# A sparse-attention kernel whose index scores take their second matmul on half of the array's rows, two heads at a time

## The chip, the core and the metric

The kernel runs on one core of a Trainium2 chip. TensorE (PE in the profile) multiplies matrices on an array of 128 rows and 128 columns: a weight load (PEld) brings one operand into the array, a matmul streams the other through it and writes to PSUM, which has 8 banks here of 128 x 512 float32. VectorE (DVE), ScalarE (ACT) and GpSimd (POOL) work on elements; SyncE (SP) and other engines issue DMAs. The metric is the device time of one execution in microseconds (us); smaller is better. The kernel before takes 1685.8 us (median of 3 runs, 1685.49 to 1687.46).

## The reference

One layer on 512 frames with 2048 channels: a norm, one wide projection, a sparse-attention mixer, a retention mixer, gates, output projections and a final norm. The change touches the part that scores keys for the sparse attention. Each query has 16 index heads of 64 numbers, all heads share one key of 64 numbers per frame, and the 128 best keys of each query are kept:

```python
score = jnp.einsum('bqhd,bsd->bqsh', qi_c, ki)
index = jnp.einsum('bqsh,bqh->bqs', jax.nn.relu(score), w_c).astype(jnp.float32)
admissible = jnp.arange(L) < limit
index = jnp.where(admissible[None, None, :], index, -jnp.inf)
_, sel = lax.top_k(index, topk)
```

A chunk of 64 queries sees only the keys up to its own end, so the kernel's block t of 128 queries needs 128 (t + 1) keys. For block 0 nothing is scored, since it has no more than 128 keys.

## The kernel before

Float32 numbers are split into a high part, rounded to the format that TensorE multiplies in one pass, and a low part, the rest. A product of two such numbers is taken as three matmuls (high by high, low by high, high by low).

The index queries of two heads come as one tile of 128 channels by 512 frames (`ps_iq`, L197 to L199, 48 matmuls of 384 columns for each of 8 tiles). `iq_split` (L434) makes two operands of it, each with 128 rows: `ta` holds the first head's high part in rows 0 to 63 and its low part in rows 64 to 127; `tz` holds the second head's low part in rows 0 to 63 and its high part in rows 64 to 127. The keys stand twice, in both halves of the rows, as a high part `ikh` and a low part `ikl`. So one matmul of `ta` with `ikh` adds high by high and low by high, and one with `ikl` adds high by low and low by low. `index_score` (L581) does these two for one head and one block t = 1, 2, 3, with 256, 384 or 512 columns, into one PSUM bank (`ps_is`); ACT takes the ReLU (L589), and VectorE weights it and adds it into `isc` (L594, L596). That is 16 heads x 3 blocks = 48 calls.

The order of the work is written out by the kernel: the engines' queues hold instructions in the order in which the program issues them. After each group of matmuls of a main product (three in the projections here) it calls `step()` (L165), which issues what is due by its own delay (`later`), and then takes one entry from a list `todo`; where that entry is None or the list is empty, it may take one entry from a background list `bg`, here at every second step. `index_tile` (L598) puts three None and six calls on `todo` for each tile. The calls lag behind: they are issued from 72 us to 131 us of the span, first between the matmuls of the further index queries, from 97 us on between those of the first value projection (`values`, L714; `ps_vn`, L725 to L727, 512 columns each, four PSUM banks held throughout). There the background list is filled as well: it loads and normalizes the input again (L680) and makes combinations of it (L275, L277), and later finds the best keys and makes the position bias.

The weights come by DMA, are split by ACT (`wh`, L137) and VectorE (`wl`, L142), and are ordered three units ahead of their use (`split_to`, L122).

One other place uses part of the array: the bias matmuls (`bias_mm`, L651) write four strips of 32 columns at a time, in eleven batches between full matmuls from 522 to 1006 us.

Of the kernel before, what the change touches and what calls it, by code (L numbers as in the profile page):

```python
# [14 lines left out]
AF = mybir.ActivationFunctionType  # L15
OP = mybir.AluOpType
# [5 lines left out]
NT = L // 128  # L22
# [13 lines left out]
def block_kernel(tc, xT, pT, posb, posq, w_in, w_v, w_ik, w_a, w_b, w_o, w_ple, w_gate,  # L36
                 w_gt, w_pt, fgb, tab, gains, cst, dec, out, out_a, out_b):
    nc = tc.nc
    pe, dve, act, pool, sp = nc.tensor, nc.vector, nc.scalar, nc.gpsimd, nc.sync

    with contextlib.ExitStack() as ctx:
# [10 lines left out]
        def U(name, dt=F32):  # L52
            return up.tile([128, L], dt, name=name, tag="u")

        def B(name, dt=F32):
            return bp.tile([128, 1280], dt, name=name, tag="b")

        def P(name):
            return pp.tile([128, L], F32, name=name, tag="p")
# [4 lines left out]
        def tok(t):  # L64
            return slice(128 * t, 128 * t + 128)
# [88 lines left out]
        todo = collections.deque()  # L154
# [52 lines left out]
        def gemm(ids, parts, name, c=ALL, order=None):  # L207
            return gemms([(ids, slice(0, 128), parts, c, name)], order=order)[0]
# [110 lines left out]
        for h in range(NH):  # L319
            u_r.append(block_pair(col(RQ, h), col(RK, h)))  # L320
            for n in (2 * h, 2 * h + 1):
                g, m = ((GB, 2 * n), (GA, 2 * n - 16))[n >= 8]
# [19 lines left out]
        for k in range(KT):  # L342
            if k in (1, 2, 4, 8, 12):
                load_to(state["raw"] + 1)
            if k < 10:
                t = U("xk")
                sp.dma_start(t, xT[:, k, :])
                xs.append(t)
            elif k % 2 == 0:
                t = B("xk2")  # L350
# [83 lines left out]
        def iq_split(ps):  # L434
            ta = U("ta", F32R)
            tz = U("tz", F32R)
            act.activation(ta[0:64, 128:], ps[0:64, 128:], AF.Copy)
            act.activation(tz[64:128, 128:], ps[64:128, 128:], AF.Copy)
            dve.tensor_sub(ta[64:128, 128:], ps[0:64, 128:], ta[0:64, 128:].bitcast(F32))
            dve.tensor_sub(tz[0:64, 128:], ps[64:128, 128:], tz[64:128, 128:].bitcast(F32))  # L440
            return ta, tz
# [4 lines left out]
        ix = iq_split(ps_iq0)  # L446
# [13 lines left out]
        wq = cp.tile([128, NT, 16], F32, name="wq")  # L460
# [117 lines left out]
        later(120, f_rope2)  # L578


        def index_score(n, lhsT, t):  # L581
            ikh, ikl = R["ik"]
            ln = 128 * (t + 1)
            ps = P("ps_is")
            q = lhsT[:, tok(t)]
            pe.matmul(ps[:, :ln], q, ikh[:, :ln], start=True, stop=False)
            pe.matmul(ps[:, :ln], q, ikl[:, :ln], start=False, stop=True)
            rl = U("relu")
            act.activation(rl[:, :ln], ps[:, :ln], AF.Relu)  # L589
            if n == 0 and t == 1:  # L590
                R["isc"] = B("isc")
            a = R["isc"][:, IOFF[t]:IOFF[t] + ln]
            if n == 0:
                dve.tensor_scalar(a, rl[:, :ln], wq[:, t, n:n + 1], None, op0=OP.mult)  # L594
            else:
                dve.scalar_tensor_tensor(a, rl[:, :ln], wq[:, t, n:n + 1], a, op0=OP.mult, op1=OP.add)  # L596

        def index_tile(m, ix):  # L598
            todo.extend(N3)
            for s in range(2):  # L600
                for t in range(1, NT):
                    todo.append(lambda s=s, t=t: index_score(2 * m + s, ix[s], t))

        index_tile(0, ix)
        for m in range(1, 8):
            ix = iq_split(gemm(u_iq[m], hparts, "ps_iq", slice(128, L)))
            index_tile(m, ix)
# [106 lines left out]
        def values(ids, name, each=lambda s: None):  # L714

            pss = [P("ps_vn") for _ in range(NT)]
            seq = ksteps(ids)
            for s, (i, k) in enumerate(seq):
                if k == 0:
                    split_to(i + AHEAD)  # L720
                    load_to(i + AHEAD + LOADS)
                h, l = loaded[i]
                a, b = hparts[s]
                for t in range(NT):
                    pe.matmul(pss[t], a[:, tok(t)], h[:, k], start=(s == 0), stop=False)  # L725
                    pe.matmul(pss[t], a[:, tok(t)], l[:, k], start=False, stop=False)  # L726
                    pe.matmul(pss[t], b[:, tok(t)], h[:, k], start=False, stop=(s == KT - 1))  # L727
                    step()
                each(s)
            return pss  # L730
# [123 lines left out]
        def x_load(count):  # L854
            while x_wanted and count:
                n, k = x_wanted.popleft()
                Xh[n][k] = U("h" + n, F32R)
                sp.dma_start(Xh[n][k].bitcast(F32), x_at[n, k])
                count -= 1
# [4 lines left out]
        for i in range(2):  # L864
            pss = values(u_av[i], "av", lambda s, i=i: x_load(2 if i else 1 + s % 2))
            vs = [normal(ps, "av", t, F32 if t == NT - 1 else F32R) for t, ps in enumerate(pss)]
            for t in range(NT - 1):
                vl = U("avl", F32R)
                dve.scalar_tensor_tensor(vl, pss[t], R["nat"][:, t:t + 1], vs[2 * t].bitcast(F32), op0=OP.mult,
                                         op1=OP.subtract)  # L870
# [28 lines left out]
        for h in range(NH):  # L899
            gate_pair(u_r[h], retention(h))  # L900
            for n in (2 * h, 2 * h + 1):
                d, m = ((sgb, 2 * n), (sga, 2 * n - 16))[n >= 8]
# [185 lines left out]
        for m in PAIRED:  # L1088
            t = B("sm")
            s, o = t[:, 0:512], t[:, 512:1024]  # L1090
# [17 lines left out]
        for m in range(8):  # L1108
# [13 lines left out]
            if m == 7:  # L1122
                todo.extend([None] * 24)
                for k in range(2):
                    t = U("pk")
# [9 lines left out]
        for m in range(MF):  # L1135
# [5 lines left out]
            ps = P("ps_pw")  # L1141
            for k in range(2):
                a, b = pparts[k]
# [5 lines left out]
            t = U("pw")  # L1149
# [31 lines left out]
        for m in range(MF):  # L1181
            pw = pws[m]
            pg = gemm(u_e[m], rparts, "ps_pg", order=R_ORDER if m == 0 else None)
            s = U("sg")
# [84 lines left out]
        s = U("sg")  # L1269
# [12 lines left out]
        rl = cp.tile([128, 1], F32, name="rl")  # L1282
# [9 lines left out]
        for q in range(MF // 4):  # L1292
            o = U("yo")
            for i in range(4):
                m = 4 * q + i
# [116 lines left out]
```

## Time and profile before

| | |
|---|---|
| Median of 3 runs | 1685.8 us |
| The profiled execution's own time | 1687.2 us |
| Its span, first to last instruction | 1685.4 us |
| TensorE busy | 1671.8 us |
| VectorE busy | 1275.0 us |
| ScalarE busy | 864.1 us |
| Index-score matmuls, busy in 71 to 131 us | 24.4 us (lengths that overlap) |

A row of the timeline gives the start in us, the length, the engine, the line of the code, the operation, what is written and read, the part of the array (128\*128 is all of it), and the shape of the operand. The rows of groups give how many there were, the busy time and the mean length in ns, and the engine's idle time ahead of them with what ended it. Lengths of matmuls overlap: what a matmul costs in a steady flow is the distance to the next one's start.

### The profile page before, as it was taken

Reading aid. Unit: us, or ns where it says so; the run is one execution under the profiler, and the core shown is the slowest. Engines: PE = TensorE matmul, PEld = TensorE weight load, DVE = VectorE, ACT = ScalarE, POOL = GpSimd, SP = SyncE. Lnnn points to the kernel's source line nnn. Section 1 sums busy time; section 2 is a strip of 40 time slices with the busy share of each in tenths; the row PEclk is TensorE's granted clock in tenths of the full one; section 3 lists DMA queues with packets and bytes.
Section 4 is the critical chain, followed back from the end, with each engine's and each line's share of the span. In section 5 each row is a group of like instructions: output and inputs, shape, how many; then the busy total and the mean of one; then the engine's idle time right before and its main releaser. Section 6 shows DMA issues by size and latency. Waiting matters only on the chain.

```text
span 1685.4 us, 24772 instructions
## 1 busy us (share of the span) xinstructions
PE 1671.8 (99%) x9208; PEld 1450.6 (86%) x9208; DVE 1275.0 (76%) x2020; ACT 864.1 (51%) x1278; POOL 213.0 (13%) x216
## 2 busy tenths in 40 slices
PE   9999999999999999999999999999999999999997
PEld 7988888888888888888888888888888888888896
DVE  7787988887887887887887776787768877864453
ACT  7465523555555555555655555566644444463342
POOL 3100000111111111111331111100000111112222
PEclk9999999999999999999999999999999999999999
DMA  7438989788787788788989889898566788733223
GB/s 288 125 101 296 364 320 327 188 223 221 169 225 198 194 223 225 172 211 219 256 235 234 222 201 244 242 370 283 176 200 189 190 230 215 204 116 100 88 63 100
DMA packets 135368, 355.85 MB, mean 211 GB/s; under 512 B 14800, under 2 KB 27088, under 8 KB 135248
## 3 DMA queue, kind: packets, MB, share of 16 engines
q1 hardware_dynamic: 102640, 256.22, 44.8%
q0 software_dynamic: 21376, 77.60, 25.2%
q10 hardware_dynamic: 11232, 20.45, 3.3%
q8 instruction: 72, 1.18, 0.3%
q14 instruction: 48, 0.39, 0.1%
HBM read 301.26 MB, written 52.95 MB: 210 GB/s over the span
## 4 chain that ended last, share of the span: by engine, by line
PE 92%; DVE 3%; ACT 2%; DMA 2%; issue 1%; SPq 0%; POOL 0%; DVEq 0%; ACTq 0%; POOLq 0%
PE ps_p L259 23%; PE ps_v L259 15%; PE ps_r L259 8%; PE ps_q L259 7%; PE ps_vn L726 3%; PE ps_vn L725 3%; PE ps_vn L727 3%; PE ps_w L197 3%; PE ps_w L198 3%; PE ps_w L199 3%; PE ps_pg L199 3%; PE ps_pg L197 3%; PE ps_pg L198 3%; DMA wraw<-w_in 1%; PE ps_iq L197 1%; PE ps_iq L199 1%
## 5 line engine op out<-in xcount | busy, mean ns | idle before, releaser
L142 DVE TENSOR_TENSOR wl<-wraw,wh 128x1024 fp32r<-128x1024 f32 (+2 forms) x459 | 560.1, 1228 | 203.5 <-ACT wh L137 198.7
L137 ACT ACTIVATE wh<-wraw 128x1024 fp32r<-128x1024 f32 (+2 forms) x459 | 474.0, 1042 | 276.3 <-DVE wraw L144 130.2
L105 POOL DMA_DIRECT2D wraw<-w_in x120 | 106.1, 957 | 841.0 <-DVE wl L142 427.3
L225 ACT ACTIVATE e<-ps_p 128x512 f32<-128x512 f32 x144 | 86.1, 598 | 157.9 <-PE ps_p L259 155.7
L259 PE MATMUL ps_p<-hs,wh 128*128 128x512 f32 x640 | 161.4, 394 | 0.0
L259 PEld LDWEIGHTS ps_p<-hs,wh 128*128 128x128 f32 x640 | 114.9, 189 | 21.3 <-issue 0.7
L725 PE MATMUL ps_vn<-wh,hh 128*128 128x512 f32 x256 | 99.8, 390 | 0.0
L727 PE MATMUL ps_vn<-wh,hl 128*128 128x512 f32 x256 | 99.7, 389 | 0.0
L726 PE MATMUL ps_vn<-wl,hh 128*128 128x512 f32 x256 | 99.7, 389 | 0.0
L259 PE MATMUL ps_p<-hs,wl 128*128 128x256 f32 x640 | 92.1, 284 | 0.0
L259 PEld LDWEIGHTS ps_p<-hs,wl 128*128 128x128 f32 x640 | 83.1, 192 | 0.5 <-issue 0.4
L259 PE MATMUL ps_r<-hs,wh 128*128 128x512 f32 x320 | 82.5, 396 | 0.7 <-ACT wh L137 0.7
L259 PE MATMUL ps_p<-ha,wh 128*128 128x512 f32 x320 | 80.4, 393 | 0.0
L259 PE MATMUL ps_v<-ha,wh 128*128 128x512 f32 x320 | 80.3, 392 | 0.0
L259 PE MATMUL ps_q<-ha,wh 128*128 128x512 f32 x320 | 80.1, 392 | 0.0
L259 PE MATMUL ps_v<-hs,wh 128*128 128x512 f32 x320 | 79.3, 389 | 0.0
L199 PE MATMUL ps_pg<-rh,wl 128*128 128x512 f32 x192 | 74.8, 390 | 0.0
L197 PE MATMUL ps_pg<-rh,wh 128*128 128x512 f32 x192 | 74.7, 389 | 0.0
L198 PE MATMUL ps_pg<-rl,wh 128*128 128x512 f32 x192 | 74.7, 389 | 0.0
L886 DVE TENSOR_TENSOR go<-e_t 128x256 f32<-128x256 f32 x160 | 68.0, 425 | 5.6
L259 PEld LDWEIGHTS ps_v<-hs,wh 128*128 128x128 f32 x320 | 60.0, 188 | 12.7 <-issue 0.2
L259 PEld LDWEIGHTS ps_v<-ha,wh 128*128 128x128 f32 x320 | 59.4, 188 | 12.4 <-issue 0.3
(361 smaller groups left out, 3495.1 us busy)
## 6 DMA issues: line engine op xcount, KB each, us to landing
wraw<-w_in SPq DMA_DIRECT2D x174, 512.0 KB, 5.6
wraw<-w_in POOLq DMA_DIRECT2D x120, 512.0 KB, 8.0
wraw<-w_v SPq DMA_DIRECT2D x32, 512.0 KB, 5.5
wraw<-w_o SPq DMA_DIRECT2D x32, 512.0 KB, 5.0
wraw<-w_o POOLq DMA_DIRECT2D x24, 512.0 KB, 6.3
wraw<-w_gate SPq DMA_DIRECT2D x24, 512.0 KB, 3.7
hd<-hs SPq DMA_DIRECT2D x32, 256.0 KB, 4.8
hs<-hd SPq DMA_DIRECT2D x32, 256.0 KB, 5.6
```

Of the source, the lines that this page charges most:

```text
L105: pool.dma_start(out=raw_tiles[r], in_=src[:, k0:k0 + 8, :], accum_op=OP.add)
L137: act.activation(h, raw, AF.Copy)
L142: dve.tensor_sub(l, raw, h.bitcast(F32))
L197: pe.matmul(o, h[:, k, w], a, start=(s == order[0]), stop=False)
L198: pe.matmul(o, h[:, k, w], b, start=False, stop=False)
L199: pe.matmul(o, l[:, k, w], a, start=False, stop=(s == order[-1]))
L225: act.activation(E[n], src, AF.Copy)
L259: pe.matmul(o[:, c], w[:, k], X[PRODUCTS[n]][k][:, c], start=(n < 4 and part == 0 and k == 0), stop=(part == parts[1] and k == 7), skip_gr ...
L725: pe.matmul(pss[t], a[:, tok(t)], h[:, k], start=(s == 0), stop=False)
L726: pe.matmul(pss[t], a[:, tok(t)], l[:, k], start=False, stop=False)
L727: pe.matmul(pss[t], b[:, tok(t)], h[:, k], start=False, stop=(s == KT - 1))
L886: dve.tensor_add(o[:, q], c0, c1)
```

## The change

`index_score` becomes `index_scores`, for both heads of a tile at once: 24 calls instead of 48. The first matmuls of the two heads stay as they are, one behind the other into two banks. The second matmuls, with the low keys, take only the 64 rows that hold the head's high part: rows 0 to 63 for the first head, rows 64 to 127 for the second, each in its own half of the array's rows (`tile_position`). The product of low query and low key is no longer added. ReLUs and accumulations of both heads follow. On `todo` each call is followed by a None, so that a tile takes nine entries as before.

```diff
-        def index_score(n, lhsT, t):
+        def index_scores(m, ix, t):
             ikh, ikl = R["ik"]
             ln = 128 * (t + 1)
-            ps = P("ps_is")
-            q = lhsT[:, tok(t)]
-            pe.matmul(ps[:, :ln], q, ikh[:, :ln], start=True, stop=False)
-            pe.matmul(ps[:, :ln], q, ikl[:, :ln], start=False, stop=True)
-            rl = U("relu")
-            act.activation(rl[:, :ln], ps[:, :ln], AF.Relu)
-            if n == 0 and t == 1:
+            pss = [P("ps_is") for s in range(2)]
+            for s, ps in enumerate(pss):
+                pe.matmul(ps[:, :ln], ix[s][:, tok(t)], ikh[:, :ln], start=True, stop=False, skip_group_check=True)
+            for s, ps in enumerate(pss):
+                r = slice(64 * s, 64 * s + 64)
+                pe.matmul(ps[:, :ln], ix[s][r, tok(t)], ikl[r, :ln], start=False, stop=True, tile_position=(64 * s, 0),
+                          skip_group_check=True)
+            if m == 0 and t == 1:
                 R["isc"] = B("isc")
             a = R["isc"][:, IOFF[t]:IOFF[t] + ln]
...
+            for s, ps in enumerate(pss):
+                n = 2 * m + s
+                rl = U("relu")
+                act.activation(rl[:, :ln], ps[:, :ln], AF.Relu)
...
         def index_tile(m, ix):
             todo.extend(N3)
-            for s in range(2):
-                for t in range(1, NT):
-                    todo.append(lambda s=s, t=t: index_score(2 * m + s, ix[s], t))
+            for t in range(1, NT):
+                todo.extend([lambda t=t: index_scores(m, ix, t), None])
```

More of the change, by code (lines that the diff above doesn't have):

```diff
@@ L578, in block_kernel @@
         later(120, f_rope2)
-        def index_score(n, lhsT, t):
+        def index_scores(m, ix, t):
             ikh, ikl = R["ik"]
             ln = 128 * (t + 1)
-            ps = P("ps_is")
-            q = lhsT[:, tok(t)]
-            pe.matmul(ps[:, :ln], q, ikh[:, :ln], start=True, stop=False)
-            pe.matmul(ps[:, :ln], q, ikl[:, :ln], start=False, stop=True)
-            rl = U("relu")
-            act.activation(rl[:, :ln], ps[:, :ln], AF.Relu)
-            if n == 0 and t == 1:
+            pss = [P("ps_is") for s in range(2)]
[6 more added lines that the diff above has]
+            if m == 0 and t == 1:
                 R["isc"] = B("isc")
             a = R["isc"][:, IOFF[t]:IOFF[t] + ln]
[L593 to L596, printed above, removed]
+            for s, ps in enumerate(pss):
+                n = 2 * m + s
+                rl = U("relu")
+                act.activation(rl[:, :ln], ps[:, :ln], AF.Relu)
+                if n == 0:
+                    dve.tensor_scalar(a, rl[:, :ln], wq[:, t, n:n + 1], None, op0=OP.mult)
+                else:
+                    dve.scalar_tensor_tensor(a, rl[:, :ln], wq[:, t, n:n + 1], a, op0=OP.mult, op1=OP.add)
         def index_tile(m, ix):
             todo.extend(N3)
-            for s in range(2):
-                for t in range(1, NT):
-                    todo.append(lambda s=s, t=t: index_score(2 * m + s, ix[s], t))
+            for t in range(1, NT):
+                todo.extend([lambda t=t: index_scores(m, ix, t), None])
         index_tile(0, ix)
```

## The prediction

> **What bounds the kernel.** I read the page's first and fourth parts, then TensorE's waits, then the timeline around the index scores.
>
> ```profile
> span 1685.4 us, 24772 instructions
> PE 1671.8 (99%) x9208; PEld 1450.6 (86%) x9208; DVE 1275.0 (76%) x2020; ACT 864.1 (51%) x1278; POOL 213.0 (13%) x216
> ...
> PE 92%; DVE 3%; ACT 2%; DMA 2%; issue 1%; SPq 0%; POOL 0%; DVEq 0%; ACTq 0%; POOLq 0%
> ```
>
> ```profile
> engine line waited for: us in total, times, longest us
> PE ps_b L1287 <- POOL rl L1283: 3.7, 1, 3.7
> PE ps_warm L381 <- DVE warm L376: 1.4, 1, 1.4
> PE ps_r L259 <- ACT wh L137: 0.7, 2, 0.5
> ...
> ```
>
> TensorE is busy 99% of the span and carries 92% of the chain that ended last. Its largest wait is in the kernel's tail (L1287), the next before the first real matmul (L381); between them it hardly waits for anybody. So a microsecond that TensorE issues more or less in the index scores goes straight into the span, as long as the other engines still keep ahead of it.
>
> The stage in question, in the timeline of TensorE (start, length, then the instruction):
>
> ```profile
> 85.92 0.28 PE L587 MATMUL ps_is<-ikl,ta 128*128 128x256 f32 x1
> 86.04 0.34 PE L197 MATMUL ps_iq<-hh,wh 128*128 128x384 f32 x1
> ...
> 86.74 0.33 PE L587 MATMUL ps_is<-ikl,ta 128*128 128x384 f32 x1
> 86.91 0.33 PE L197 MATMUL ps_iq<-hh,wh 128*128 128x384 f32 x1
> ...
> 87.66 0.40 PE L587 MATMUL ps_is<-ikl,ta 128*128 128x512 f32 x1
> 87.89 0.34 PE L197 MATMUL ps_iq<-hh,wh 128*128 128x384 f32 x1
> ```
>
> ```profile
> L587 PE MATMUL ps_is<-ikl,ta x24: 278/335/397, 72.1 to 127.2; 128*128 128x256 f32 x8, 128*128 128x384 f32 x8, 128*128 128x512 f32 x8
> L587 PE MATMUL ps_is<-ikl,tz x24: 278/336/397, 74.7 to 130.3; 128*128 128x256 f32 x8, 128*128 128x384 f32 x8, 128*128 128x512 f32 x8
> ```
>
> Matmuls overlap, so the price of one is the distance from its start to the next start, not its length: 0.12, 0.17 and 0.23 us for 256, 384 and 512 columns. No weight load shows up between them: each is done beside the matmul ahead of it.
>
> **What the change removes.** 48 second matmuls (two heads, eight tiles, three query blocks) become 24 concurrent pairs, each on the two row halves. If a pair costs what one costs now, the saving is 24 matmuls: 8 x (0.12 + 0.17 + 0.23) = 8 x 0.52 = 4.16 us. It is on the path: there is no other work under it. Number and size of all other matmuls stay.
>
> **What it adds: 24 changes of the array's shape and 24 back.** Every pair stands between full 128*128 matmuls. The trace has no row-half matmul; the nearest rows are those of the bias matmuls at L651, which use the array in four column strips (128*32) amid full matmuls. TensorE's rows around one such batch, and the weight loads:
>
> ```profile
> 799.98 0.39 PE L259 MATMUL ps_v<-ha,wh 128*128 128x512 f32 x1
> 800.30 0.34 PE L651 MATMUL ps_bias<-mk,d 128*32 128x384 f16 x1
> 800.80 0.34 PE L651 MATMUL ps_bias<-mk,d 128*32 128x384 f16 x4
> 801.07 0.50 PE L259 MATMUL ps_v<-ha,wh 128*128 128x512 f32 x1
> 801.40 0.40 PE L259 MATMUL ps_v<-ha,wh 128*128 128x512 f32 x1
> ```
>
> ```profile
> 800.30 0.09 PEld L651 LDWEIGHTS <-d 128*32 128x32 f16 x1 [0.35 <-issue]
> 801.07 0.19 PEld L259 LDWEIGHTS ps_v<-ha,wh 128*128 128x128 f32 x1 [0.32 <-issue]
> ```
>
> Going in: the last full matmul has 512 columns, so the next should start 0.23 us on; it starts 800.30 - 799.98 = 0.32 us on, 0.09 late. Its weight load isn't ahead of it as usual, but starts with it, after 0.35 us in which the loader waited for nothing that the profile names: the array was run empty first. Coming back: the batch's matmuls come four at a time every (800.80 - 800.30) / 3 = 0.17 us; the full one comes 0.27 us after the last four began (0.01 of it is their spread), so again 0.09 late. Then its weight load lies open too: that matmul takes 0.50 us against 0.39 ahead of the batch, and the next comes 801.40 - 801.07 = 0.33 us on, not 0.23. So a crossing costs 0.09 us for the emptying and about 0.11 us for a load of 128 columns that nothing hides. The first and the last batch show the same way back (here 256 columns, 0.12 us apart in steady flow):
>
> ```profile
> 522.97 0.39 PE L259 MATMUL ps_p<-hs,wl 128*128 128x256 f32 x1
> 523.20 0.40 PE L259 MATMUL ps_p<-hs,wl 128*128 128x256 f32 x2
> ```
>
> ```profile
> 1005.95 0.39 PE L259 MATMUL ps_p<-hs,wl 128*128 128x256 f32 x1
> 1006.17 0.40 PE L259 MATMUL ps_p<-hs,wl 128*128 128x256 f32 x2
> ```
>
> Both times 0.22 to 0.23 us to the next start, 0.11 too many.
>
> For the new pairs I take 0.09 + 0.11 into the half shape and 0.09 + 0.11 out of it: 0.40 us a call, 24 x 0.40 = 9.6 us. What is unknown, with its ends. The emptying: 0 (as between two matmuls of one shape) to 0.09; I take 0.09, since the row is a change of shape as here. The load going in: about 0.01 (the 32-column load: 0.34 us for the batch's first matmul as for its last) to 0.11 for one of 128 columns; the new loads have 128 columns on 64 rows, so I take 0.11, for both halves at once, since the four strips' loads and matmuls start together (one row, x4, 0.34 us long). If the two load one after the other, another 0.11 us a call, 2.6 us. If the halves' matmuls don't run at once, no saving at all, 4.16 us.
>
> The Trainium skill's page "TensorE: Matmul & The Clock Gate" (LDWEIGHTS) says that a load's time goes by its columns, columns / 1.2 ns, and not by its rows; that makes 107 ns for the half-row loads too, and by it the sum stays as it is, where half the time for half the rows would take 24 x 0.05 = 1.3 us off. The measured 0.11 us agrees for full rows; no run yet shows 64.
>
> **What it moves.** A pair's two ReLUs, and VectorE's two accumulations, are now queued together, and the first head's second matmul ends one matmul later than before, as the other head's first lies ahead of it. ACT has room:
>
> ```profile
> PE ps_is L587: 20.4, 33
> ```
>
> ```profile
> 104.05 1.28 ACT L563 ACT_TABLE_LOAD   x1
> ...
> 108.68 0.86 ACT L589 ACTIVATE relu<-ps_is 128x512 f32<-128x512 f32 x2
> ```
>
> ACT was waiting for L587 ahead of 33 of the 48 ReLUs, so later releases cost nothing there. Each call takes two PSUM banks at once instead of one; beside the four banks of the value projection four are left, two calls' worth. The one place where ReLUs lag is the sine table's load: the calls issued from 104.05 on get their ReLUs by 109.5. If a pair had to wait for a bank there, it would be at most these 3 us, once. I cost it at nothing, since three to four steps without a call (12 matmuls of 0.23 us) follow each three calls, and TensorE waited for nobody there.
>
> The list gets None behind each call instead of further calls; the number of slots (9 a tile) is the same, so index calls end where they did. But from 98 us on the background list fills every second empty slot: in the changed program's order six background steps more lie ahead of the index scores' end. By VectorE's order these are two normalizations (L680) and eleven 128x256 operations such as L277's:
>
> ```profile
> L277 DVE TENSOR_TENSOR hs<-t,hs 128x256 fp32r<-128x256 f32 x25 | 9.1, 417 | 0.0
> L680 DVE SCALAR_TENSOR_TENSOR xn<-xn,g_sb,r_b 128x512 f32<-128x512 f32 x12 | 8.4, 744 | 0.0
> ```
>
> ```profile
> 98.00:131.00 33.00, 33.00 (x156) 27.74 (x155) 28.06 (x48) 20.88 (x40) 0.00 (x0) 1.00 0.41 132
> ```
>
> That is 2 x 0.744 + 11 x 0.417 = 6.1 us, in a stretch where VectorE (third busy column) has 33.00 - 28.06 = 4.9 us free and half of the added time, some 2.7 us, comes to it: 34.2 us of work in 35.7. The cover is thin. The weights' low halves (L142) stand in the same queue; they are ordered three weight units ahead, and a unit of the value projection is 24 matmuls of 0.23 us, so being 5 us late still costs nothing. The stores, loads and bias batches behind it come some steps earlier; their number stays. I cost all this at nothing.
>
> **Sum.** 24 x 0.40 - 4.16 = +5.4 us on a span of 1685.4. The profiled execution itself took 1687.2 us, the median of the three runs is 1685.8; added to the median: 1691.2 us, 0.32% more. About 0.2% (3.4 us) can be told from no change.
>
> **Rivals.**
> *The array takes the row halves without emptying or open loads (faster).* The saving of 4.16 us stands alone: 1681.6 us. It decides if a crossing costs less than 4.16 / 48 = 0.087 us; to be seen as faster it has to be under 0.02. For it: inside a bias batch the strips follow each other with nothing lost, and no row shows row halves. Against: both directions of the bias batches cost 0.09 before any load. 9%. The page named above, in "Packing small matmuls", lets small-K matmuls in different row groups run at once, starts at most 4 ns apart, which by itself would be this saving; the strips' starts agree with it, but its examples stay in one shape.
>
> *The loads are fetched ahead, only the emptying stays (same).* 48 x 0.09 - 4.16 = +0.2 us, 1686.0; with the open load on the way out alone, +2.8 us. For it: all loads in steady flow are hidden. Against: in both load rows of the batch the loader stood idle 0.32 to 0.35 us. 11%. The page's "The mechanism" has loads pulled ahead of matmuls where row groups differ or the spare weight buffer is free; a full matmul uses all row groups, so by that only the second half's load could be early.
>
> *The halves load or run one after the other (slower still).* +8.0 us with serial loads, +9.6 us with serial matmuls (whose second load then hides): 1693.8 to 1695.4. For it: the strips split columns, and rows may share a path. Against: nothing measured. 13%.
>
> *VectorE becomes the bound from 98 to 131 us.* It asks for more than two units' lead, about 11 us, to be used up; the price is what it lacks, 2 to 3 us on top: 1693.5. 5%.
>
> **The numbers.** My forecast has 62%: 1691.2, of itself 1689 to 1693 (half-time loads take 1.3 off; the rows' rounding of 0.01 us is 0.5 us over 48 crossings, and there are two terms in each). Faster 9%, same 11%, slower 62 + 13 + 5 = 80%. The range runs from the emptying alone, 1686.0, to serial halves, 1695.4; the faster rival is left out.
>
> **What would show it.** In the changed kernel's timeline: the two L591 matmuls start within some ns of each other; the first starts about 0.09 us later than steady flow behind L588's second, and is about 0.11 us longer than one of its columns; the matmul behind the pair likewise. From L588's first start to the start of the second matmul behind a 512-column call it is about 4 x 0.23 + 0.40 = 1.32 us where that stage's matmuls have 512 columns too, against 5 x 0.23 = 1.15 now. Stretch 71 to 98 us grows by 2 to 3 us with the same matmuls, and the same again to 131; nothing after it. Wrong if loads lie ahead of the pair, if L591's starts are 0.1 us or more apart, or if TensorE waits for a wl or a ReLU.

## The result and the profile after

| | before | after |
|---|---|---|
| Median of 11 runs each | 1686.21 us | 1690.62 us |
| Profiled execution's span | 1685.4 us | 1688.7 us |
| Its own time | 1687.2 us | 1690.44 us |

The changed kernel takes 1.0024 times as long, with a 95% interval of 1.0017 to 1.0032: 4.4 us slower at the medians. The forecast was 5.4 us. The profiled execution of before was 1.0 us above its median, so its span and the one after differ by less than the medians do.

TensorE around a call of 512 columns, in the timeline of the changed kernel (start, length, instruction):

```profile
90.26 0.39 PE L588 MATMUL ps_is<-ikh,ta 128*128 128x512 f32 x1
90.49 0.40 PE L588 MATMUL ps_is<-ikh,tz 128*128 128x512 f32 x1
90.81 0.49 PE L591 MATMUL ps_is<-ikl,ta 64*128 64x512 f32 x1
90.82 0.49 PE L591 MATMUL ps_is<-ikl,tz 64*128 64x512 f32 x1
91.24 0.45 PE L197 MATMUL ps_iq<-hh,wh 128*128 128x384 f32 x1
91.52 0.34 PE L198 MATMUL ps_iq<-hl,wh 128*128 128x384 f32 x1
```

and the weight loads beside them:

```profile
90.26 0.19 PEld L588 LDWEIGHTS ps_is<-ikh,tz 128*128 128x128 f32 x1
90.81 0.18 PEld L591 LDWEIGHTS ps_is<-ikl,ta 64*128 64x128 f32 x1 [0.36 <-issue]
90.81 0.18 PEld L591 LDWEIGHTS ps_is<-ikl,tz 64*128 64x128 f32 x1
91.24 0.19 PEld L197 LDWEIGHTS ps_iq<-hh,wh 128*128 128x128 f32 x1 [0.24 <-issue]
```

The two half-row matmuls start together. The first comes 0.32 us behind the last full one, 0.09 later than in steady flow, and is 0.49 us long, not 0.39: its load lies open. The way back looks the same: L197 is 0.45 us long, not 0.33, and the next matmul starts 0.28 us behind it, not 0.17. From the first L588 to L198 it is 1.26 us; in steady flow three matmuls of 512 columns and one of 384 take 3 x 0.23 + 0.17 = 0.86. The round trip costs 0.40 us. Beside the value projection, where the neighbours have 512 columns too, the same stretch takes 1.32 us (106.51 to 107.83 us), the figure that was forecast.

TensorE's waits are fewer than before:

```profile
PE ps_b L1293 <- POOL rl L1289: 3.7, 1, 3.7
PE ps_warm L381 <- DVE warm L376: 1.4, 1, 1.4
PE ps_ikw L199 <- DVE wl L142: 0.4, 1, 0.4
PE ps_pt L997 <- ACT bm L988: 0.2, 1, 0.2
```

So TensorE waits for no other engine in the index scores, and the wait for `wh` at L259 (0.7 us in the profile of before) is gone.

With landmarks in the two traces (the starts of the same matmuls) the span splits into stages. Stage 1 runs from the first L494 matmul (a transpose of the keys) to the first of the value projection, stage 2 to the first matmul of `ps_v`, and stage 3 from there to the end of the paired products (the first `ps_w`):

| | stage 1 | stage 2 | stage 3 |
|---|---|---|---|
| before | 31.04 | 182.83 | 826.01 |
| before, profiled a second time | 31.04 | 182.83 | 824.90 |
| after | 33.59 | 185.40 | 824.10 |

Stages 1 and 2 hold all 24 calls, twelve in each, and grew by 2.55 + 2.57 = 5.1 us. Stage 3 shrank by 0.8 us against the second profile.

### The profile page after: what moved, and what is told of

It reads as the page before. It is cut to its first block, busy times and chain, and to the rows that moved or that the text cites. A ratio compares the mean times of both kernels' runs of the same rounds, so it can differ in the third digit from the quotient of the medians.

```text
span 1688.7 us, 24776 instructions
## 1 busy us (share of the span) xinstructions
PE 1676.8 (99%) x9208; PEld 1447.5 (86%) x9208; DVE 1277.4 (76%) x2020; ACT 861.9 (51%) x1278; POOL 213.6 (13%) x216
## 4 chain that ended last, share of the span: by engine, by line
PE 95%; DVE 2%; ACT 1%; DMA 1%; issue 0%; SPq 0%; POOL 0%; DVEq 0%; ACTq 0%
PE ps_p L259 24%; PE ps_v L259 16%; PE ps_r L259 8%; PE ps_q L259 8%; PE ps_vn L731 4%; PE ps_vn L733 3%; PE ps_vn L732 3%; PE ps_w L197 3%; PE ps_w L198 3%; PE ps_w L199 3%; PE ps_pg L199 3%; PE ps_pg L198 3%; PE ps_pg L197 3%; PE ps_iq L197 1%; PE ps_iq L198 1%; PE ps_iq L199 1%
## 5 line engine op out<-in xcount | busy, mean ns | idle before, releaser
L259 PE MATMUL ps_p<-hs,wh 128*128 128x512 f32 x640 | 160.9, 393 | 0.0
L259 PEld LDWEIGHTS ps_p<-hs,wh 128*128 128x128 f32 x640 | 115.0, 189 | 20.5
L731 PE MATMUL ps_vn<-wh,hh 128*128 128x512 f32 x256 | 100.9, 394 | 0.0
L259 PE MATMUL ps_p<-hs,wl 128*128 128x256 f32 x640 | 92.0, 284 | 0.0
L259 PEld LDWEIGHTS ps_p<-hs,wl 128*128 128x128 f32 x640 | 83.1, 192 | 0.4 <-issue 0.4
L259 PE MATMUL ps_r<-hs,wh 128*128 128x512 f32 x320 | 82.4, 395 | 0.0
L259 PE MATMUL ps_q<-ha,wh 128*128 128x512 f32 x320 | 80.5, 393 | 0.0
L259 PE MATMUL ps_v<-ha,wh 128*128 128x512 f32 x320 | 80.3, 392 | 0.0
L259 PE MATMUL ps_p<-ha,wh 128*128 128x512 f32 x320 | 80.1, 392 | 0.0
L259 PE MATMUL ps_v<-hs,wh 128*128 128x512 f32 x320 | 79.2, 389 | 0.0
L198 PE MATMUL ps_pg<-rl,wh 128*128 128x512 f32 x192 | 74.7, 389 | 0.0
L197 PE MATMUL ps_pg<-rh,wh 128*128 128x512 f32 x192 | 74.7, 389 | 0.0
L259 PEld LDWEIGHTS ps_v<-hs,wh 128*128 128x128 f32 x320 | 60.0, 188 | 12.8 <-issue 0.3
L259 PEld LDWEIGHTS ps_v<-ha,wh 128*128 128x128 f32 x320 | 59.4, 188 | 12.2 <-issue 0.2
```

What stands on the lines that cost most here:

```text
L197: pe.matmul(o, h[:, k, w], a, start=(s == order[0]), stop=False)
L198: pe.matmul(o, h[:, k, w], b, start=False, stop=False)
L259: pe.matmul(o[:, c], w[:, k], X[PRODUCTS[n]][k][:, c], start=(n < 4 and part == 0 and k == 0), stop=(part == parts[1] and k == 7), skip_gr ...
```

## The experiments

**The kernel before once more**, without an edit, for a second profile.

> The kernel before once more, for a second profile of it. Between the two profiles TensorE lost 0.5 us at 308 us and 1.0 us at 560 us in the kernel before (waits of L259 for the weights' high half wh) that the changed one does not have. If these waits belong to the order of the work, they stand in this profile too, at the same places and with the same lengths; if they are a matter of one execution, they are elsewhere or gone. Time: no change, 1.000 within 0.1%.

Measured: ratio 1.0002 (0.9993 to 1.0011). Of the two waits one remains, at 308 us:

```profile
PE ps_r L259 <- ACT wh L137: 0.2, 1, 0.2
```

The loss at 560 us, about 1 us, is not there. So the first profile of before had it by chance, and what belongs to the order of the work is the smaller wait.

**An entry that does nothing in place of None**, so that background work stays where it was:

```diff
-                todo.extend([lambda t=t: index_scores(m, ix, t), None])
+                todo.extend([lambda t=t: index_scores(m, ix, t), lambda: None])
```

> The changed kernel with an empty entry that does nothing in place of each None behind a call, so that the background list is not taken from there: background work stands against the matmuls as in the kernel before. Theory: the crossings alone cost 24 x 0.40 - 4.16 = 5.4 us (the index stretch of the changed kernel measured 5.1), and the moved background work gave some 0.5 to 1.5 us back; so 5.1 to 6.0 us over the kernel before. Rival: the moved background work is worth nothing: 4.4 us over it, as the changed kernel.

Measured: 1691.35 us against 1686.18 (ratio 1.0031, 1.0020 to 1.0043): 5.2 us, 0.7 more than the changed kernel. The intervals of the two overlap, so the stages have to tell: stages 1 and 2 are the same as after (33.59 and 185.40 us), stage 3 is 824.90 as in the second profile of before, with the wait of 0.2 us at L259 back. That wait costs more than its length. Here is the place with the empty entries,

```profile
312.68 0.28 PE L259 MATMUL ps_q<-ha,wl 128*128 128x256 f32 x1
313.20 0.73 PE L259 MATMUL ps_r<-hs,wh 128*128 128x512 f32 x2 [0.24 <-ACT wh L137]
313.78 0.35 PE L780 MATMUL ps_rs<-go 128*128 128x128 f32 x1
```

and in the changed kernel:

```profile
312.46 0.28 PE L259 MATMUL ps_q<-ha,wl 128*128 128x256 f32 x1
312.58 0.63 PE L259 MATMUL ps_r<-hs,wh 128*128 128x512 f32 x2
313.05 0.28 PE L780 MATMUL ps_rs<-go 128*128 128x128 f32 x1
```

From `ps_q` to `ps_rs` it is 1.10 us there and 0.59 here. So the round trips cost 5.1 us, and the background work that comes some steps earlier gives 0.8 us back in stage 3, 0.5 of it at this one place.

**All 128 rows for the second matmuls**, in the order of the changed kernel:

```diff
-                r = slice(64 * s, 64 * s + 64)
-                pe.matmul(ps[:, :ln], ix[s][r, tok(t)], ikl[r, :ln], start=False, stop=True, tile_position=(64 * s, 0),
-                          skip_group_check=True)
+                pe.matmul(ps[:, :ln], ix[s][:, tok(t)], ikl[:, :ln], start=False, stop=True, skip_group_check=True)
```

> The order of the changed kernel (both heads in one call, None behind it), but the second matmuls on all 128 rows as before, so that no shape changes in the index scores. Theory: the index stretch is as long as in the kernel before, so all of its loss lies in the crossings; what is left is the moved background work, 0 to -1.5 us. Rival: the pairing itself (two banks at once, ReLUs two by two) costs some of the 5 us; then this is slower than the kernel before by that part.

Measured: ratio 1.0004 (0.9995 to 1.0013), no difference. Stage 1 takes 30.95 us, as before; stage 3 824.11, as after. Stage 2 is 0.5 us longer than before: here TensorE waited for a bank, which it did not in the changed kernel.

```profile
117.48 0.39 PE L731 MATMUL ps_vn<-wh,hl 128*128 128x512 f32 x1
117.86 0.44 PE L588 MATMUL ps_is<-ikh,ta 128*128 128x384 f32 x1
118.35 0.45 PE L588 MATMUL ps_is<-ikh,tz 128*128 128x384 f32 x1
118.63 0.34 PE L590 MATMUL ps_is<-ikl,ta 128*128 128x384 f32 x1
```

The second L588 comes 0.49 us behind the first, and the first 0.38 behind L731, where 0.17 and 0.23 are usual. ACT shows why:

```profile
115.96 0.42 ACT L275 ACTIVATE hs<-t 128x256 fp32r<-128x256 f32 x1 [2.06 <-DVE t L288]
116.28 1.04 ACT L137 ACTIVATE wh<-wraw 128x1024 fp32r<-128x1024 f32 x1
117.23 1.06 ACT L597 ACTIVATE relu<-ps_is 128x512 f32<-128x512 f32 x2
```

A background cast (L275) stood ahead of the ReLUs and had waited 2.06 us for VectorE; the second ReLU ends at 118.29 us, 0.06 ahead of the second L588. The cast is background work, which comes earlier in this order than in the kernel before. The changed kernel has the same order and does not wait: there the cast and the ReLUs come 1.4 us later, but the call that needs the banks comes 4.2 us later (122.08 us), since TensorE has lost time by then. Without the wait this order would, by its stages, be ahead of the kernel before by under 1 us, less than can be told.

**Both heads on the same half of the rows:**

```diff
-                r = slice(64 * s, 64 * s + 64)
-                pe.matmul(ps[:, :ln], ix[s][r, tok(t)], ikl[r, :ln], start=False, stop=True, tile_position=(64 * s, 0),
+                r = slice(0, 64)
+                pe.matmul(ps[:, :ln], ix[s][r, tok(t)], ikl[r, :ln], start=False, stop=True, tile_position=(0, 0),
```

> The second matmuls of both heads in the same half of the rows, 0 to 63 (so for the second head it is the low part of the query with the low part of the key that is added). Same crossings, but the two cannot run at once. Theory: the pair's concurrency is worth 8 x 0.52 = 4.16 us, so 8.5 us over the kernel before, 4.2 over the changed one. Rival: the two halves run one behind the other in the changed kernel too: no difference from it, 4.4 us over the kernel before.

Measured: 1695.33 us, ratio 1.0053 (1.0041 to 1.0066), 9.1 us over before and 4.7 over the changed kernel by medians. Stages 1 and 2 grew by 4.3 us on the changed kernel (35.86 and 187.44). The second matmul now starts 0.33 us behind the first instead of beside it:

```profile
92.66 0.50 PE L591 MATMUL ps_is<-ikl,ta 64*128 64x512 f32 x1
92.99 0.39 PE L591 MATMUL ps_is<-ikl,tz 64*128 64x512 f32 x1
```

0.33 is 0.10 for the open load of the first plus 0.23 for its columns; the second is 0.39 us long, its load is hidden. So the two halves do run at once in the changed kernel, and the saving of 4.16 us is real.

**Half rows without pairs:** the kernel before with its second matmul alone on 64 rows, 48 round trips.

```diff
-            pe.matmul(ps[:, :ln], q, ikl[:, :ln], start=False, stop=True)
+            r = slice(64 * (n % 2), 64 * (n % 2) + 64)
+            pe.matmul(ps[:, :ln], lhsT[r, tok(t)], ikl[r, :ln], start=False, stop=True, tile_position=(64 * (n % 2), 0),
+                      skip_group_check=True)
```

> The kernel before, one head a call, with its second matmul on the 64 rows of the high query alone: 48 ways there and back, each for one half-row matmul, nothing concurrent, nothing saved, background work as in the kernel before. Theory: 48 x 0.40 = 19.2 us over the kernel before. Rival (the 0.40 us belong to a pair, 0.20 to each half): 9.6 us.

Measured: 1705.46 us against 1686.28, ratio 1.0115 (1.0099 to 1.0130): 19.2 us. The price belongs to the round trip, not to the half.

**Fewer round trips, three ways.** In each, a call takes its banks, does all its full matmuls, then all its half-row ones, then the ReLUs. Blocks 2 and 3 of a tile in one call:

```diff
+            todo.extend([lambda: index_scores(m, ix, (1,)), None])
+            todo.extend([lambda: index_scores(m, ix, (2, 3)), None, None, None])
```

> Blocks 2 and 3 of a tile in one call (four banks): their four full matmuls, then their four half-row matmuls, so 16 crossings there and back instead of 24, with the same matmuls. Theory (a fixed price of 0.40 us for each way there and back): the index stretch gains 8 x 0.40 = 3.2 us on the changed kernel, which leaves it 1.9 us longer than in the kernel before, and with the moved background work some 1.2 us over it in all. A call takes all four banks that the value projection leaves, so a wait for a ReLU may eat part of it. Rival (the price goes with the number of half-row matmuls, as for loads that never hide): 4.4 us over the kernel before, as the changed one.

The same block of two tiles in one call:

```diff
+                for t in range(1, NT):
+                    todo.extend([lambda t=t: index_scores(tiles, t)] + [None] * 5)
```

> The same block of two tiles in one call (four banks), so 12 crossings there and back, the same matmuls, slots as before. Theory: index stretch 12 x 0.40 - 4.16 = 0.6 us longer than in the kernel before (0.3 by the changed kernel's measured 5.1 instead of 5.4); background work comes earlier still, worth 0 to -1 us, and waits for banks may add some: -0.7 to +1 us over the kernel before. Rival (price by half-row matmul): 4.4 us over it.

And all three blocks of a tile in one call, for the first four tiles alone:

```diff
+            if m < 4:
+                todo.extend([lambda: index_scores(m, ix, (1, 2, 3))] + [idle] * 5)
+            else:
+                for t in range(1, NT):
+                    todo.extend([lambda t=t: index_scores(m, ix, (t,)), idle])
```

> As the run with the empty entries (background work as in the kernel before, one call a block), but for the first four tiles, which are scored between the index-query matmuls where six banks are free, all three blocks stand in one call: six full matmuls, then six half-row ones. So 4 + 12 = 16 crossings there and back instead of 24, without a background entry moved and without the last four banks being taken. Theory: 8 x 0.39 = 3.1 us less than the run with the empty entries, that is 2.0 us over the kernel before; no wait of TensorE in the index scores. Rival (the price goes with the half-row matmuls, or calls with more banks wait whatever the place): 5.1 us over the kernel before, or more.

Measured: 1697.30 us (ratio 1.0064, 1.0051 to 1.0077), 1694.15 (1.0048, 1.0035 to 1.0061) and 1688.14 (1.0012, 1.0003 to 1.0021). The first two are slower than the changed kernel, against the expectation; the third is 2.2 us over before where 2.0 was expected.

Stage 1, where banks are plenty, decides on the price. The last column takes 0.39 us a round trip, the figure that fits the rows best, less 2.08 us (half of 4.16) where the halves run at once:

| kernel | round trips in stage 1 | stage 1, us over before | 0.39 each, less saving |
|---|---|---|---|
| all rows | 0 | -0.09 | 0 |
| one call for three blocks | 4 | -0.60 | -0.52 |
| two tiles | 6 | 0.24 | 0.26 |
| two blocks | 8 | 1.04 | 1.04 |
| after | 12 | 2.55 | 2.60 |
| same half | 12 | 4.82 | 4.68 |
| single heads | 24 | 9.26 | 9.36 |

The number of half-row matmuls is the same in all but the first row; only the round trips differ, and pairing. Inside one shape loads hide: in the first of the three, the second pair starts 0.28 us behind the first (0.10 open load and 0.17 for 384 columns) and has its plain length.

```profile
74.54 0.44 PE L592 MATMUL ps_is<-ikl,ta 64*128 64x384 f32 x1
74.55 0.44 PE L592 MATMUL ps_is<-ikl,tz 64*128 64x384 f32 x1
74.82 0.39 PE L592 MATMUL ps_is<-ikl,ta 64*128 64x512 f32 x1
```

What the first two lost beyond that lies mostly in stage 2, beside the value projection, where a call of four banks needs every free one: there they are 5.8 us (two blocks) and 7.1 us (two tiles) over what the same sum gives. In the two-blocks kernel:

```profile
115.78 0.72 PE L588 MATMUL ps_is<-ikh,ta 128*128 128x512 f32 x1 [2.07 <-ACT relu L601]
116.30 0.63 PE L588 MATMUL ps_is<-ikh,tz 128*128 128x512 f32 x1
```

TensorE stood 2.07 us for a ReLU, and then its matmuls were 0.63 to 0.72 us long instead of 0.39. The stretches around it (busy times of TensorE, loads, VectorE, ScalarE, GpSimd; then the granted clock):

```profile
112.00:116.00 4.00, 1.93 (x9) 1.34 (x8) 3.40 (x6) 1.74 (x5) 0.00 (x0) 0.99 0.00 0
116.00:119.30 3.30, 3.30 (x9) 1.95 (x9) 3.13 (x8) 1.98 (x6) 0.00 (x0) 0.50 0.46 166
119.30:123.00 3.70, 3.70 (x18) 3.03 (x17) 3.49 (x7) 2.35 (x6) 0.00 (x0) 1.00 0.70 234
```

The wait is paid twice: 2 us of standing, and about 1.7 us because the clock is halved for the 3.4 us that follow (115.9 to 119.3 us). Waits of 1.3 us at 104 us and of 0.3 us at 135 us, for banks as well, come on top. The two-tiles kernel has one wait of 2.51 us, and the matmuls behind it, of 256 columns, start 0.49 us apart instead of 0.12:

```profile
117.77 0.39 PE L588 MATMUL ps_is<-ikh,ta 128*128 128x256 f32 x1 [2.51 <-ACT relu L599]
118.26 0.38 PE L588 MATMUL ps_is<-ikh,tz 128*128 128x256 f32 x1
```

Its half clock begins at 120.2 us, and it lost about 1.4 us more at 166 and 173 us, where TensorE waited for `wl`. The two-blocks kernel lost another 4 us in stage 3, with waits for `wh` (1.7 us at 812 us) and `wl` (0.7 us at 821 us) where weights came late; that its background work stands two operations earlier than in the changed kernel may be the cause, but nothing here shows it. In the third kernel, which takes many banks only where they are free and moves no background work, TensorE waits for no bank, and the time is the expected one within its interval (0.5 to 3.5 us over before).

## Why the prediction was right, point by point

- *What bounds the kernel.* Right. What TensorE issued more came through: 5.1 us in stages 1 and 2, nothing under other work.
- *The saving of 4.16 us.* Right: 4.3 us with the same-half kernel. The halves start together, as the column strips did.
- *The round trip at 0.40 us.* Right: 0.40 in the quoted call, 0.39 by the table over 4 to 24 round trips. The emptying (0.09) and the open load (0.10) were both carried over from the bias matmuls, although those split columns and these rows. The rivals without emptying, with loads fetched ahead, and with serial halves are out.
- *The load of 64 rows at 0.11 us.* Right: the first half-row matmul is 0.10 us longer than it would be. The rule in the Trainium skill's page "TensorE: Matmul & The Clock Gate" (LDWEIGHTS), that a load's time goes by columns and not by rows, agrees with it.
- *Stages 1 and 2 together at +5.4.* Measured 5.1. Left open: 0.3 us, 0.01 us a call.
- *The moved background work at nothing.* This is the step that missed, and with it the forecast of nothing after the index scores: it was worth -0.8 us, shown by stage 3 of the run with the empty entries. It is why 4.4 and not 5.2 us were measured. A trace can tell that TensorE waits little; which of these small waits go away when background work moves was not to be read from it, and one of the two in the profile of before was chance.
- *VectorE as a bound.* It did not come to that in the changed kernel. From 98 to 131 us VectorE is 1.3 us busier than before:

```profile
98.00:131.00 33.00, 33.00 (x146) 24.25 (x145) 29.34 (x51) 19.73 (x41) 0.00 (x0) 1.00 0.45 152
```

That stretch ends too early to judge by, since the last accumulation into `isc` now ends at 137.8 us. Up to there VectorE does 22 background operations where the kernel before does 11, 5.3 us more. Two normalizations and nine operations of 256 columns came, not eleven, so the 6.1 us were a little high; the last accumulation ends 0.9 us later than with the empty entries, and TensorE waits for none of it.

- *Two banks a call at nothing.* Right for the changed kernel, but with less room than was argued, and for another reason: the prediction looked at the sine table's load, whereas the wait in the all-rows kernel came from a background cast that stood in ACT's queue behind VectorE. At four banks a call the same cover was gone.

## What to carry to other kernels

Half-array matmuls save only what exceeds the way into their shape and back: here 0.40 us a round trip, as much as 1.7 matmuls of 512 columns, so a single pair between full matmuls did not pay, and the four-tile kernel gained in stage 1 only by setting six half-row matmuls behind one change. The price could be read off a place of the trace where the shape changes, here even one with another kind of strip. Grouping costs PSUM banks, and one wait for a bank, 2.07 us and about 1.7 us of slow clock behind it, cost more than the four round trips that the two-blocks kernel saved in the same stage (4 x 0.39 = 1.6 us).

## What had not been expected

In the two-blocks kernel a single wait of TensorE of 2.07 us was followed by 3.4 us at half the clock, the waits of 1.3 us (104 us) and 1.7 us (812 us) in the same kernel by none. The page "TensorE: Matmul & The Clock Gate" of the Trainium skill (in "Why this matters for your kernels") warns of idle gaps over about 3 us; here a shorter one was enough. In the changed kernel the granted clock stays at 1.00 all through the index scores, so the round trips themselves, with 0.09 us of emptying each way, did not touch it.
